# One of a seven-product pair's four weight sums moves to the narrow tile ahead of unit a, and units c and d exchange their contents

## The chip, the cores and the metric

One Trainium2 chip, one of its cores. The time is the device time of one execution in microseconds (us). Engines are named as in the profile: PE multiplies matrices (PEld loads its stationary operand), DVE is the vector engine, ACT the scalar engine, POOL the general one, SP issues the loads of the weights. All of them run their own queue of instructions in order and wait for one another through semaphores.

## The reference

A decoder trunk of two layers on 256 tokens with 2048 features: layer 0 mixes tokens by gated linear attention, layer 1 by differential attention over a shared K/V, and behind each stands a SwiGLU feed-forward. Nearly all the work is in products of the 256 tokens with large weights in float32. Cut to what matters here:

```python
def swiglu(h, w_gate_up, w_down):                     # (2048, 11264), (5632, 2048)
    gate, up = jnp.split(h @ w_gate_up, 2, axis=-1)
    return (jax.nn.silu(gate) * up) @ w_down
...
    for i in range(DEPTH):                            # 2
        h = rmsnorm(x, pre_mix_g[i])
        mix = gla_mixer(h, ...) if i < N_A_LAYERS else diff_mixer(h, k_sh, v_sh, ...)
        x = x + rmsnorm(mix, post_mix_g[i])
        f = swiglu(rmsnorm(x, pre_ffn_g[i]), ffn_w_gate_up[i], ffn_w_down[i])
        x = x + rmsnorm(f, post_ffn_g[i])
```

## The kernel before

**Weights as units.** Every weight reaches the core in blocks of 128x1024 floats (512 KB), two 512-column pieces of one output chunk side by side: rows k1 = 2s in the left half, rows k2 = 2s + 1 in the right. `load` (L256) brings a block into one of five `raw` buffers. `split` (L290) turns it into two tiles that PE multiplies at full rate: ACT casts it to `hi` (L294), DVE subtracts to get `lo` (L296). A product then takes three matmuls: hi by hi, hi by lo, lo by hi (`mm_act` L361, `triple` L438). Nine `hi` and `lo` buffers of the full width form a ring, so conversion runs ahead of PE by up to nine units.

**Pairs.** Two output chunks c1, c2 of the same weight are computed together by `duo_act` (L446, gated linear attention) and `duo_apart` (L485, elsewhere). At the steps s listed in `FAST_...` (L40 to L44) the eight block products of two token halves, two row blocks and two column chunks are replaced by seven. Such a step loads two blocks, r1 (chunk c1) and r2 (chunk c2), and feeds PE four units: a (r1 as loaded, 2 products), b (sums in r2, 2 products), c (sums in r1, 2 products) and d (a tile of half width, 1 product). With L and R for the halves, the sums that `sums` (L310) writes are, in order: r1L = r1L + r2L; r2L = r2L + r2R; t2 = r1L + r2R; r1R = t2 + r1R. Unit c then holds (r1L + r2L) and the last sum, unit d holds t2 = r1L + r2L + r2R. There are 122 such pairs, 98 of them in the two feed-forwards. The products go to seven accumulators ("banks"): 4 belongs to r1L + r2L, 5 to r1L + r2L + r2R. Token forms that go with them are made once for each stage by `build_forms` (L538); `early` and `late` of each stage combine the banks.

**What sets the order.** `take` (L349) asks for units in the order of `weight_stream` (L81); `pump` (L342) converts ahead as far as the ring allows and then issues loads ahead, up to five blocks beyond those done with. A raw buffer is filled again when the last instruction that reads the block in it has finished, so a load waits in SP's queue for a `split` on DVE. `convert` (L325) calls `sums` when it comes to unit b. A scheduler then puts the instructions of each engine in a fixed order, by what it reckons to be ready first; it moves matmuls, splits and sums past one another. The tile t2 lay in the stage's own pool (`self.narrow[0]`), the half-width `hi` and `lo` of unit d in that pool or in two or three spare places (`room`).

Of the kernel before, what the change touches and what calls it, by code (L numbers as in the profile page):

```python
# [11 lines left out]
F32 = mybir.dt.float32  # L12
# [3 lines left out]
ALU = mybir.AluOpType  # L16
AX = mybir.AxisListType

P = 128
# [3 lines left out]
C = 512  # L23
# [163 lines left out]
class Trunk:  # L187
# [119 lines left out]
        )  # L307
        return hi

    def sums(self):  # L310

        nc = self.nc
        r1, r2 = self.pending
        t2 = self.narrow[0].tile([P, C], F32, tag="sum", name=self.uid("sum"))

        def add(out, in0, in1):
            nc.vector.tensor_tensor(out=out, in0=in0, in1=in1, op=ALU.add)  # L317

        add(r1[:, :C], r1[:, :C], r2[:, :C])
        add(r2[:, :C], r2[:, :C], r2[:, C:])  # L320
        add(t2, r1[:, :C], r2[:, C:])
        add(r1[:, C:], t2, r1[:, C:])
        self.pending = r1, r2, t2

    def convert(self):  # L325
        n = self.n_conv
        kind = self.stream[n][2]
        self.n_done += kind in ("plain", "beside", "c", "b")
        if kind == "plain":
            self.subs[n] = self.split(self.raw(), n in self.pool_lo) if n else self.split_halves(self.raw())  # L330
        elif kind == "beside":
            self.subs[n] = self.split_beside(self.raw())
        elif kind == "a":
            self.pending = self.raw(), self.raw()
            self.subs[n] = self.split(self.pending[0])
        else:
            if kind == "b":
                self.sums()
            self.subs[n] = self.split(self.pending["cbd".index(kind)])
        self.n_conv += 1  # L340

    def pump(self):  # L342
# [103 lines left out]
    def duo_act(self, aT, forms, fast, c1, c2, early, late):  # L446

        ps = [self.acc() for _ in range(6)] + [self.tp().rearrange("p j t -> p (j t)")]
        for s in range(8):
            k1, k2 = 2 * s, 2 * s + 1  # L450
            if s in fast:
                f = forms.pairs.index(s)
                plan = {
                    "a": ((0, (k1, 0)), (1, (k2, 0))),
                    "b": ((6, (f, 2)), (2, (f, 3))),
                    "c": ((4, (f, 0)), (3, (k2, 1))),
                    "d": ((5, (f, 1)),),
                }
                first, last = s == fast[0], s == fast[-1]
                for kind, prods in plan.items():  # L460
                    wp = self.take("duo", (c1, c2, s), kind)
                    for j, (bank, (i, which)) in enumerate(prods):
                        plain = kind == "a" or bank == 3
                        a = aT.tokens(i, which) if plain else forms.fast(i, which)
                        stop = last and bank in (0, 5, 6)
                        self.triple(ps[bank], a, wp, j, first, stop)
                    self.free()
                    if kind != "d":
                        self.tick()
                if last:  # L470
                    early(ps)
                continue
            for (w, n), pair in ((c1, ((1, 0), (3, 1))), (c2, ((4, 1), (2, 2)))):
                wp = self.take(w, (n, s))
                for bank, which in pair:
                    for j in range(2):
                        a = forms.diff(k1 + j) if which == 2 else aT.tokens(k1 + j, which)
                        self.triple(ps[bank], a, wp, j, False, s == 7 and j == 1)
                    if s == 7:
                        late(bank, ps)  # L480
                    if bank in (2, 3):
                        self.free()
                    self.tick()

    def duo_apart(self, aT, forms, fast, chunks, early, late):  # L485

        ps = {}

        def add(bank, a, wp, j, last):
            first = bank not in ps  # L490
            if first:
                ps[bank] = self.acc() if bank < 6 else self.tp().rearrange("p j t -> p (j t)")
            self.triple(ps[bank], a, wp, j, first, last)

        for s in range(8):
            k1, k2 = 2 * s, 2 * s + 1
            if s not in fast:
                for (w, n), banks in zip(chunks, ((1, 3), (2, 7))):
                    wp = self.take(w, (n, s))
                    for b, bank in enumerate(banks):  # L500
                        for j in range(2):
                            add(bank, aT.tokens(k1 + j, b), wp, j, s == 7 and j == 1)
                        if b:
                            self.free()
                        if s == 7:
                            late(bank, ps)
                        self.tick()
                continue
            f, last = forms.pairs.index(s), s == fast[-1]
            plan = {  # L510
                "a": ((0, aT.tokens(k1, 0)), (1, aT.tokens(k2, 0))),
                "b": ((6, forms.fast(f, 2)), (2, forms.fast(f, 3))),
                "c": ((4, forms.fast(f, 0)), (3, aT.tokens(k2, 1))),
                "d": ((5, forms.fast(f, 1)),),
            }
            for kind, prods in plan.items():
                wp = self.take("duo", (*chunks, s), kind)
                for j, (bank, a) in enumerate(prods):
                    add(bank, a, wp, j, last and bank in (0, 4, 5, 6))
                self.free()  # L520
                if kind != "d":
                    self.tick()
            if last:
                early(ps)
# [1059 lines left out]
```

## Time and profile before

| what | before |
|---|---|
| time, median of 3 runs (2179.7 to 2179.91) | 2179.7 us |
| span of the profiled execution | 2177.2 us |
| PE busy, matmuls | 99%, 10098 |
| PEld busy | 83% |
| DVE busy, instructions | 89%, 2646 |
| ACT busy | 58% |
| DMA engines' packets of the weight queue, share of 16 engines | 60.2% |
| mean granted clock of PE | 0.999 |

The span runs from the first to the last instruction of one profiled execution; the time of a run is about 2.5 us more. A row of the chain or of a group names a line of the kernel, an engine, an operation, "out<-in" by tile names without numbers, a count, the busy time and the mean duration. A matmul's duration in the trace contains its way through the array, so consecutive matmuls overlap: their starts tell the rate. DVE instructions overlap a little as well: one of 690 ns lets the next start 600 to 720 ns after it.

### The profile page before, as it was taken

Reading aid. Unit: us, or ns where it says so; the run is one execution under the profiler, and the core shown is the slowest. Engines: PE = TensorE matmul, PEld = TensorE weight load, DVE = VectorE, ACT = ScalarE, POOL = GpSimd, SP = SyncE. Lnnn points to the kernel's source line nnn. Section 1 sums busy time; section 2 is a strip of 40 time slices with the busy share of each in tenths; the row PEclk is TensorE's granted clock in tenths of the full one; section 3 lists DMA queues with packets and bytes.
Section 4 is the critical chain, followed back from the end, with each engine's and each line's share of the span. In section 5 each row is a group of like instructions: output and inputs, shape, how many; then the busy total and the mean of one; then the engine's idle time right before and its main releaser. Section 6 shows DMA issues by size and latency. Waiting matters only on the chain.

```text
span 2177.2 us, 28399 instructions
## 1 busy us (share of the span) xinstructions
PE 2162.6 (99%) x10098; PEld 1798.1 (83%) x10098; DVE 1932.7 (89%) x2646; ACT 1267.2 (58%) x1744; POOL 35.6 (2%) x66
## 2 busy tenths in 40 slices
PE   9999999999999999999999999999999999999998
PEld 8887788888888888888878888888888888888886
DVE  7989988998999999998898567889999999999986
ACT  8656665665655555554676455556566555555553
POOL 1000000000000000000000000000000000000000
PEclk9999999999999999999999999999999999999999
DMA  8545566666655566665757655465656555666664
GB/s 309 169 149 191 177 228 213 213 221 215 228 176 199 194 213 213 194 224 189 243 187 248 186 174 161 151 235 189 231 194 223 182 185 195 209 206 212 212 213 135
DMA packets 123315, 440.09 MB, mean 202 GB/s; under 512 B 13899, under 2 KB 16628, under 8 KB 121380
## 3 DMA queue, kind: packets, MB, share of 16 engines
q1 hardware_dynamic: 121996, 436.44, 60.2%
q10 hardware_dynamic: 1176, 1.84, 0.3%
q8 instruction: 79, 1.29, 0.2%
q14 instruction: 64, 0.52, 0.1%
HBM read 429.82 MB, written 9.97 MB: 202 GB/s over the span
## 4 chain that ended last, share of the span: by engine, by line
PE 96%; DVE 2%; DMA 1%; issue 1%; ACT 1%; POOL 0%; SPq 0%; DVEq 0%; POOLq 0%; ACTq 0%
PE acc L444 13%; PE acc L443 13%; PE acc L442 13%; PE acc L372 10%; PE acc L370 10%; PE acc L371 10%; PE acc L585 8%; PE acc L586 4%; PE tp L443 3%; PE tp L444 3%; PE tp L442 3%; PE tp L606 1%; DVE lo L296 1%; PE acc L1307 0%; PE acc L1346 0%
## 5 line engine op out<-in xcount | busy, mean ns | idle before, releaser
L294 ACT CAST hi<-raw 128x1024 fp32r<-128x1024 f32 x905 | 929.5, 1051 | 656.6 <-DVE raw L317 272.7
L296 DVE TENSOR_TENSOR lo<-raw,hi 128x1024 fp32r<-128x1024 f32 x903 | 1077.6, 1220 | 151.8 <-ACT hi L294 148.9
L370 PE MATMUL acc<-hi,f_ffn_gT 128*128 128x512 f32 x704 | 274.1, 390 | 0.0
L371 PE MATMUL acc<-lo,f_ffn_gT 128*128 128x512 f32 x704 | 274.0, 390 | 0.0
L372 PE MATMUL acc<-hi,f_ffn_gT 128*128 128x512 f32 x704 | 268.9, 389 | 0.0
L444 PE MATMUL acc<-hi,h_ffn 128*128 128x512 f32 x666 | 259.6, 390 | 0.0
L443 PE MATMUL acc<-lo,h_ffn 128*128 128x512 f32 x666 | 259.2, 389 | 0.0
L442 PE MATMUL acc<-hi,h_ffn 128*128 128x512 f32 x666 | 258.4, 390 | 0.0
L372 PEld LDWEIGHTS acc<-hi,f_ffn_gT 128*128 128x128 f32 x704 | 132.2, 188 | 27.3
L370 PEld LDWEIGHTS acc<-hi,f_ffn_gT 128*128 128x128 f32 x704 | 132.2, 188 | 27.2
L371 PEld LDWEIGHTS acc<-lo,f_ffn_gT 128*128 128x128 f32 x704 | 132.2, 188 | 27.0
L444 PEld LDWEIGHTS acc<-hi,h_ffn 128*128 128x128 f32 x666 | 125.0, 188 | 26.5 <-issue 0.6
L443 PEld LDWEIGHTS acc<-lo,h_ffn 128*128 128x128 f32 x666 | 125.1, 188 | 25.9
L442 PEld LDWEIGHTS acc<-hi,h_ffn 128*128 128x128 f32 x666 | 125.0, 188 | 25.9
L585 PE MATMUL acc<-h_q,hi 128*128 128x512 f32 x256 | 92.5, 401 | 0.0
L585 PE MATMUL acc<-h_kv,hi 128*128 128x512 f32 x256 | 90.6, 399 | 0.0
L585 PE MATMUL acc<-h_mix,hi 128*128 128x512 f32 x256 | 90.5, 398 | 0.0
L317 DVE TENSOR_TENSOR raw<-sum,raw 128x512 f32<-128x512 f32 x122 | 84.2, 690 | 3.5
L317 DVE TENSOR_TENSOR raw<-raw 128x512 f32<-128x512 f32 x122 | 84.2, 690 | 3.3
L317 DVE TENSOR_TENSOR raw<-raw,raw 128x512 f32<-128x512 f32 x122 | 83.9, 687 | 2.0
L317 DVE TENSOR_TENSOR sum<-raw,raw 128x512 f32<-128x512 f32 x122 | 83.5, 684 | 0.0
L586 PE MATMUL acc<-h_q,lo 128*128 128x256 f32 x256 | 73.2, 286 | 0.0
(416 smaller groups left out, 3912.4 us busy)
## 6 DMA issues: line engine op xcount, KB each, us to landing
raw<-in_w_gu_dram SPq DMA_DIRECT2D x352, 512.0 KB, 4.4
raw<-in_w_d_dram SPq DMA_DIRECT2D x176, 512.0 KB, 5.2
raw<-in_gla_w_r_dram SPq DMA_DIRECT2D x32, 512.0 KB, 4.4
raw<-in_gla_w_v_dram SPq DMA_DIRECT2D x32, 512.0 KB, 4.0
raw<-in_gla_w_out_dram SPq DMA_DIRECT2D x32, 512.0 KB, 4.5
raw<-in_w_v_dram SPq DMA_DIRECT2D x32, 512.0 KB, 4.7
raw<-in_w_k_dram SPq DMA_DIRECT2D x32, 512.0 KB, 4.0
raw<-in_diff_w_q_dram SPq DMA_DIRECT2D x32, 512.0 KB, 3.5
```

The lines of the kernel that those rows point to most:

```text
L294: nc.scalar.copy(hi, src)
L296: eng.tensor_tensor(out=lo, in0=src, in1=hi.bitcast(F32), op=ALU.subtract)
L317: nc.vector.tensor_tensor(out=out, in0=in0, in1=in1, op=ALU.add)
L370: nc.tensor.matmul(ps, ah, rh, start=(kt == 0), stop=False)
L371: nc.tensor.matmul(ps, ah, rl, start=False, stop=False)
L372: nc.tensor.matmul(ps, al, rh, start=False, stop=(kt == 2 * ns - 1))
L442: nc.tensor.matmul(ps, ah, wh, start=first, stop=False)
L443: nc.tensor.matmul(ps, ah, wl, start=False, stop=False)
L444: nc.tensor.matmul(ps, al, wh, start=False, stop=last)
L585: nc.tensor.matmul(ps, lh, aT.both(kt), start=(kt == 0), stop=False)
L586: nc.tensor.matmul(ps[:, SEQ:], ll, aT.hi(kt), start=False, stop=(kt == KT - 1))
L606: nc.tensor.transpose(tp[:, j, :], src[:, j * P : (j + 1) * P], self.ident)
```

## The change

`sums` is gone. `convert_fast` now makes the first sum when it comes to unit a, out of the place: t1 = r1L + r2L into a tile of half width, and only then splits r1. At unit b it makes r2L = r2L + r2R, r1L = t1 + r2R, r1R = r1L + r1R. So r1 then holds in its left half what t2 held, and the half-width tile holds r1L + r2L: unit c feeds bank 5 (and 3), unit d bank 4. The tile comes from the ring's pool, with one buffer for the whole kernel. The number of sums, splits, loads and matmuls stays as it was. What differs is the order, and which engine waits for what.

```diff
-    def sums(self):
-        nc = self.nc
-        r1, r2 = self.pending
-        t2 = self.narrow[0].tile([P, C], F32, tag="sum", name=self.uid("sum"))
...
-        add(r1[:, :C], r1[:, :C], r2[:, :C])
-        add(r2[:, :C], r2[:, :C], r2[:, C:])
-        add(t2, r1[:, :C], r2[:, C:])
-        add(r1[:, C:], t2, r1[:, C:])
-        self.pending = r1, r2, t2
+    def add(self, out, in0, in1):
+        self.nc.vector.tensor_tensor(out=out, in0=in0, in1=in1, op=ALU.add)
+
+    def convert_fast(self, kind):
+        if kind == "a":
+            r1, r2 = self.raw(), self.raw()
+            t1 = self.ring.tile([P, C], F32, tag="sum", name=self.uid("sum"), bufs=1)
+            self.pending = r1, r2, t1
+            self.add(t1, r1[:, :C], r2[:, :C])
+            return self.split(r1)
+        r1, r2, t1 = self.pending
+        if kind == "b":
+            self.add(r2[:, :C], r2[:, :C], r2[:, C:])
+            self.add(r1[:, :C], t1, r2[:, C:])
+            self.add(r1[:, C:], r1[:, :C], r1[:, C:])
+            return self.split(r2)
+        return self.split(r1 if kind == "c" else t1)
...
-        elif kind == "a":
-            self.pending = self.raw(), self.raw()
-            self.subs[n] = self.split(self.pending[0])
         else:
-            if kind == "b":
-                self.sums()
-            self.subs[n] = self.split(self.pending["cbd".index(kind)])
+            self.subs[n] = self.convert_fast(kind)
...
-                    "c": ((4, (f, 0)), (3, (k2, 1))),
-                    "d": ((5, (f, 1)),),
+                    "c": ((5, (f, 1)), (3, (k2, 1))),
+                    "d": ((4, (f, 0)),),
...
-                "c": ((4, forms.fast(f, 0)), (3, aT.tokens(k2, 1))),
-                "d": ((5, forms.fast(f, 1)),),
+                "c": ((5, forms.fast(f, 1)), (3, aT.tokens(k2, 1))),
+                "d": ((4, forms.fast(f, 0)),),
```

In the changed file the sums stand at L311, and most lines have moved up by one (L296 has not; L443 of before is L442). Three places show how the scheduled order differs. Tile numbers are kept in the rows; raw_2848 and raw_2851 are the blocks r1 and r2 of one fast step of layer 1's feed-forward, raw_2854 and raw_2857 the two blocks of the plain step behind it, and raw_2863 and raw_2871 are r1 and r2 of the next fast step.

DVE before, from the last sum of the first of these steps to the first sums of the next:

```order
L317 TENSOR_TENSOR raw_2848_14954<-sum_2868_15053,raw_2848_14954 128x512
L296 TENSOR_TENSOR lo_2870_15059<-raw_2851_14966,hi_2869_15058 128x1024
L296 TENSOR_TENSOR f_ffn1_rest_13223<-sum_2868_15053,f_ffn1_rest_13223 128x512
L296 TENSOR_TENSOR lo_2873_15077<-raw_2848_14954,hi_2872_15076 128x1024
L296 TENSOR_TENSOR lo_2880_15125<-raw_2854_14978,hi_2879_15124 128x1024
L609 TENSOR_TENSOR f_ffn1_gT2_14686<-tp_2875_15082,f_ffn1_gT2_14686 128x4x128
L609 TENSOR_TENSOR f_ffn1_gT2_14686<-tp_2876_15089,f_ffn1_gT2_14686 128x4x128
L296 TENSOR_TENSOR lo_2883_15143<-raw_2857_14987,hi_2882_15142 128x1024
L296 TENSOR_TENSOR lo_2886_15163<-raw_2863_15015,hi_2885_15162 128x1024
L317 TENSOR_TENSOR raw_2863_15015<-raw_2863_15015,raw_2871_15062 128x512
```

DVE after, the same stretch:

```order
L311 TENSOR_TENSOR raw_2848_14954<-sum_2864_15033,raw_2851_14966 128x512
L296 TENSOR_TENSOR lo_2870_15059<-raw_2851_14966,hi_2869_15058 128x1024
L311 TENSOR_TENSOR raw_2848_14954<-raw_2848_14954 128x512
L296 TENSOR_TENSOR lo_2873_15077<-raw_2848_14954,hi_2872_15076 128x1024
L311 TENSOR_TENSOR sum_2885_15162<-raw_2863_15015,raw_2871_15062 128x512
L296 TENSOR_TENSOR lo_2880_15125<-raw_2854_14978,hi_2879_15124 128x1024
L296 TENSOR_TENSOR lo_2883_15143<-raw_2857_14987,hi_2882_15142 128x1024
L311 TENSOR_TENSOR raw_2871_15062<-raw_2871_15062 128x512
L296 TENSOR_TENSOR lo_2887_15165<-raw_2863_15015,hi_2886_15164 128x1024
L608 TENSOR_TENSOR f_ffn1_gT2_14686<-tp_2875_15082,f_ffn1_gT2_14686 128x4x128
L608 TENSOR_TENSOR f_ffn1_gT2_14686<-tp_2876_15089,f_ffn1_gT2_14686 128x4x128
```

The next step's first sum, which reads r2 = raw_2871, now stands ahead of the splits of the plain step (lo_2880, lo_2883) and of its own unit a; the split of unit d (f_ffn1_rest, not in the second list) has moved ahead of unit b's.

PE before at the same place, from the last matmul of unit a (lo_2865) on:

```order
L444 MATMUL acc_2895_15213<-hi_2864_15033,h_ffn1_0_13065 128x512
L442 MATMUL acc_2895_15213<-hi_2879_15124,h_ffn1_0_13065 128x512
L370 MATMUL acc_2866_15039<-hi_2849_14962,f_ffn1_gT2_14686 128x512
L371 MATMUL acc_2866_15039<-lo_2850_14963,f_ffn1_gT2_14686 128x512
L370 MATMUL acc_2877_15096<-hi_2855_14983,f_ffn1_gT2_14686 128x512
L371 MATMUL acc_2877_15096<-lo_2856_14984,f_ffn1_gT2_14686 128x512
L370 MATMUL acc_2867_15040<-hi_2849_14962,f_ffn1_gT2_14686 128x512
L371 MATMUL acc_2867_15040<-lo_2850_14963,f_ffn1_gT2_14686 128x512
L370 MATMUL acc_2878_15097<-hi_2855_14983,f_ffn1_gT2_14686 128x512
L371 MATMUL acc_2878_15097<-lo_2856_14984,f_ffn1_gT2_14686 128x512
L443 MATMUL acc_2895_15213<-lo_2880_15125,h_ffn1_0_13065 128x512
```

PE after (L605 are transposes, which before stand ahead of unit a):

```order
L443 MATMUL acc_2895_15213<-hi_2865_15035,h_ffn1_0_13065 128x512
L605 MATMUL tp_2875_15082<-ident_72,sg_2858_14989 128x128 x4
L605 MATMUL tp_2876_15089<-ident_72,sg_2858_14989 128x128 x4
L441 MATMUL acc_2895_15213<-hi_2879_15124,h_ffn1_0_13065 128x512
L441 MATMUL acc_2894_15209<-hi_2886_15164,h_ffn1_0_13065 128x512
L442 MATMUL acc_2895_15213<-lo_2880_15125,h_ffn1_0_13065 128x512
```

The first use of lo_2880 has moved ahead of eight matmuls on f_ffn1_gT2 and behind eight transposes.

The third place is the last head of differential attention. DVE before, from unit c of the first fast step of the output projection to the head's scores (s7):

```order
L296 TENSOR_TENSOR lo_2348_12378<-raw_2307_12181,hi_2347_12377 128x1024
L296 TENSOR_TENSOR lo_2369_12468<-sum_2346_12372,hi_2368_12467 128x512
L296 TENSOR_TENSOR lo_2361_12425<-raw_2304_12159,hi_2360_12424 128x1024
L1311 TENSOR_TENSOR s7_0_12397<-acc_2356_12394,bias7_12345 128x256
L1315 TENSOR_REDUCE st_2357_12399<-s7_0_12397 128x2
```

DVE after:

```order
L296 TENSOR_TENSOR lo_2348_12378<-raw_2307_12181,hi_2347_12377 128x1024
L296 TENSOR_TENSOR lo_2361_12425<-raw_2304_12159,hi_2360_12424 128x1024
L296 TENSOR_TENSOR lo_2371_12484<-raw_2313_12217,hi_2370_12483 128x1024
L311 TENSOR_TENSOR sum_2384_12538<-raw_2336_12319,raw_2349_12381 128x512
L311 TENSOR_TENSOR raw_2349_12381<-raw_2349_12381 128x512
L296 TENSOR_TENSOR lo_2376_12510<-raw_2326_12268,hi_2375_12509 128x1024
L1310 TENSOR_TENSOR s7_0_12397<-acc_2356_12394,bias7_12347 128x256
L1314 TENSOR_REDUCE st_2357_12399<-s7_0_12397 128x2
```

Two splits of plain blocks and two sums of the next fast step now stand ahead of the head's scores.

More of the change, by code (lines that the diff above doesn't have):

```diff
@@ L308, in split_beside @@
         return hi
-    def sums(self):
-        nc = self.nc
-        r1, r2 = self.pending
-        t2 = self.narrow[0].tile([P, C], F32, tag="sum", name=self.uid("sum"))
-        def add(out, in0, in1):
-            nc.vector.tensor_tensor(out=out, in0=in0, in1=in1, op=ALU.add)
-        add(r1[:, :C], r1[:, :C], r2[:, :C])
-        add(r2[:, :C], r2[:, :C], r2[:, C:])
-        add(t2, r1[:, :C], r2[:, C:])
-        add(r1[:, C:], t2, r1[:, C:])
-        self.pending = r1, r2, t2
+    def add(self, out, in0, in1):
[14 more added lines that the diff above has]
+        return self.split(r1 if kind == "c" else t1)
     def convert(self):
```

## Prediction

> **What bounds the kernel now.** The page's head comes first: the span, the busy time of each engine, and the chain of work that ended last.
>
> ```profile
> span 2177.2 us, 28399 instructions
> ...
> PE 2162.6 (99%) x10098; PEld 1798.1 (83%) x10098; DVE 1932.7 (89%) x2646; ACT 1267.2 (58%) x1744; POOL 35.6 (2%) x66
> ...
> PE 96%; DVE 2%; DMA 1%; issue 1%; ACT 1%; POOL 0%; SPq 0%; DVEq 0%; POOLq 0%; ACTq 0%
> ```
>
> PE is busy 99% and makes up 96% of the chain, but busy alone proves little, since consecutive matmuls overlap. So the waits of PE come next, the whole answer:
>
> ```profile
> PE acc L372 <- DVE h_ffn L647: 1.2, 4, 0.3
> PE acc L693 <- POOL ones L718: 1.1, 1, 1.1
> PE acc L370 <- ACT h_kv L645: 1.0, 1, 1.0
> PE acc L372 <- DVE h_kv L647: 0.9, 3, 0.4
> PE tp L641 <- DMA x_in<-in_x_dram: 0.7, 1, 0.7
> PE acc L370 <- ACT diff_oT L1370: 0.7, 1, 0.7
> PE acc L371 <- DVE lo L287: 0.2, 1, 0.2
> ```
>
> The columns are total, times and longest in us. All of PE's waits are 5.8 us, and only the last two rows have to do with weights or with work near a moved sum. No row names a `lo` of L296: PE never waits for a converted unit. That limits any gain to 5.8 us, most of which (norms, x, ones) the change doesn't touch. It limits no loss, so the question is whether DVE, which makes every `lo` in order, can now come late for PE.
>
> The stretch from 600 to 662.5 us, all of it feed-forward, shows how much DVE has in hand (columns: length, then busy time and count of PE, PEld, DVE, ACT, POOL, then clock, DMA share, GB/s):
>
> ```profile
> 600.00:662.50 62.50, 62.50 (x281) 51.84 (x281) 59.08 (x71) 35.02 (x39) 0.00 (x0) 1.00 0.60 201
> ```
>
> PE has no idle time at a granted clock of 1.00; DVE has 62.50 - 59.08 = 3.4 us.
>
> **Work removed and added: nothing, 0 us.** Four sums per pair before, four after. A unit carries as many matmuls as it did, and units c and d only exchange banks 4 and 5.
>
> ```profile
> L296 DVE TENSOR_TENSOR lo<-raw,hi 128x1024 fp32r<-128x1024 f32 x903 | 1077.6, 1220 | 151.8 <-ACT hi L294 148.9
> ...
> L317 DVE TENSOR_TENSOR raw<-raw,raw 128x512 f32<-128x512 f32 x122 | 83.9, 687 | 2.0
> ...
> L317 DVE TENSOR_TENSOR sum<-raw,raw 128x512 f32<-128x512 f32 x122 | 83.5, 684 | 0.0
> ```
>
> A sum takes 684 to 687 ns whether it writes over its input or into a tile of its own, so t1 out of place costs what the sum in place did: 122 times 3 ns, 0.4 us of DVE's time at the most, inside its idle time. The cast to `hi` of unit a no longer stands next to the sum that overwrites r1L, and ACT, which waits 272.7 us for such sums, waits less:
>
> ```profile
> ACT hi L294 <- DVE raw L317: 272.7, 84, 5.5
> ```
>
> ACT is 58% busy and absent from PE's list but for 1.7 us of other tiles; what it gains PE cannot use. I take 0.
>
> **The new wait.** t1 reads r2 before r1 is split, so DVE meets r2's transfer earlier by the splits that used to stand in between. Where r2 has only just been asked for, DVE stands, and every `lo` behind it is late. What counts is whether one of these is needed within the delay. A typical place, in the stretch above:
>
> ```profile
> 636.88 0.33 SPq L259 DMA_DIRECT2D raw<-in_w_gu_dram  x1
> ```
>
> ```profile
> 637.37 4.62 DVE L296 TENSOR_TENSOR lo<-raw,hi 128x1024 fp32r<-128x1024 f32 x4
> 642.03 0.69 DVE L317 TENSOR_TENSOR raw<-raw,raw 128x512 f32<-128x512 f32 x1
> ```
>
> r2 is issued at 636.88. With the 3.5 us that a single transfer takes (row of the next site) it is there at 640.4. Before, the first sum came at 642.0. In the changed order it stands behind the first of the four splits, at 637.37 + 4.62 / 4 = 638.5, and waits 1.9 us. By the same step on other pairs I find such a wait, 1.2 to 1.9 us, at some 40 of the 122, about one in each such stretch of feed-forward. One fits into the 3.4 us, and the unit behind it has time: the `lo` that DVE writes from 1692.83 on (below) is first read here, 16 us later.
>
> ```profile
> 1710.08 0.39 PE L443 MATMUL tp<-lo,f_ffn_fast 128*128 128x512 f32 x1
> ```
>
> So elsewhere I take 0.
>
> **The first place where it does not fit: 1690 us**, the first two places of the order lists. The load of r2 (raw_2871), how long it took to land, and DVE:
>
> ```profile
> 1694.09 0.33 SPq L259 DMA_DIRECT2D raw<-in_w_gu_dram  x1
> ```
>
> ```profile
> raw<-in_w_gu_dram SPq DMA_DIRECT2D x1, 512.0 KB, 3.5
> ```
>
> ```profile
> 1692.83 1.23 DVE L296 TENSOR_TENSOR lo<-raw,hi 128x1024 fp32r<-128x1024 f32 x1
> 1693.98 0.68 DVE L296 TENSOR_TENSOR f_ffn_rest<-sum,f_ffn_rest 128x512 fp32r<-128x512 f32 x1
> 1694.58 2.35 DVE L296 TENSOR_TENSOR lo<-raw,hi 128x1024 fp32r<-128x1024 f32 x2
> ```
>
> SP issues when unit b's split ends (1692.83 + 1.23 = 1694.06). The changed order has the same instructions ahead of that split's end and of unit c's (unit d's split has moved forward, one sum back, 0.60 us each to the next start), so the issue stays at 1694.09 and r2 lands at 1697.6. Unit c's `lo` starts at 1694.58 and takes half of the 2.35, some 1.14 to the next start; DVE then reaches t1 at 1695.72 and waits 1.9. Sum (0.65 to the next start) and split (1.22): lo_2880 is ready at 1697.6 + 0.65 + 1.22 = 1699.47. PE:
>
> ```profile
> 1697.62 0.39 PE L442 MATMUL acc<-hi,h_ffn 128*128 128x512 f32 x1
> 1697.85 0.39 PE L370 MATMUL acc<-hi,f_ffn_gT 128*128 128x512 f32 x1
> ...
> 1699.66 0.39 PE L443 MATMUL acc<-lo,h_ffn 128*128 128x512 f32 x1
> ```
>
> Before, the use is the L443 at 1699.66, eight matmuls after 1697.85, which gives 0.226 each. In the changed order these eight stand behind it, and one other matmul (on hi_2886) ahead, so PE gets there at 1699.66 - 1.81 + 0.23 = 1698.1, and waits 1699.47 - 1698.1 = **1.4 us**. Bounds: 0 if PE is late by then or r2 comes sooner, and 2.3 if r2 takes the 4.4 us that is the median over all such loads.
>
> ```profile
> raw<-in_w_gu_dram SPq DMA_DIRECT2D x352, 512.0 KB, 4.4
> ```
>
> The Trainium skill ("DMA: Bandwidth & Descriptors", section "Anatomy of one DMA", for transfers that GpSimd issues, while these come from SP) fits a transfer as a fixed 2.0 us plus bytes over 436 GB/s; for 512 KB that is an estimate of 3.2, and the stall would be 1.1. The trace's 3.5 decides. The same page's "Rules for kernel authors" says to issue a DMA early and wait on its semaphore late; a sum moved forward does the reverse of the second, and by that rule the time rises.
>
> **The second place: the last head of differential attention**, where two splits and two sums now stand ahead of the scores s7.
>
> ```profile
> 1386.77 0.42 DVE L1311 TENSOR_TENSOR s<-acc,bias 128x256 f32<-128x256 f32 x1 [0.99 <-PE acc L1307]
> ...
> 1390.30 1.22 DVE L296 TENSOR_TENSOR lo<-raw,hi 128x1024 fp32r<-128x1024 f32 x1
> ...
> 1392.15 1.22 DVE L296 TENSOR_TENSOR lo<-raw,hi 128x1024 fp32r<-128x1024 f32 x1 [0.30 <-ACT hi L294]
> ...
> 1393.88 0.48 DVE L1329 SCALAR_TENSOR_TENSOR s<-s,st 128x256 f32<-128x256 f32 x1
> ```
>
> ```profile
> 1396.90 0.38 PE L1337 MATMUL tp<-ident,s 128*128 128x128 f32 x2
> ```
>
> ```profile
> 1407.90 0.50 PE L370 MATMUL acc<-hi,diff_oT 128*128 128x512 f32 x1 [0.68 <-ACT diff_oT L1370]
> ```
>
> What now stands ahead of s7 takes 1.14 + 0.60 + 0.60 + 1.14 = 3.5; the d split that stood there (0.60) is among what comes later. The 0.99 of idle time in front of s7 takes up about that much, leaving s7 some 2.4 late. Two splits leave the stretch up to the probabilities, with 0.30 of idle time (2.57); a d split and an a split (0.60 + 1.14 = 1.74) enter. So the last probabilities end at 1393.88 + 0.48 + 2.4 - 2.57 + 1.74 = 1395.9, and PE transposes them at 1396.90: **0**. If no idle time is taken up, 1.3 more makes them 0.3 late, and with another split of 1.14 ahead 1.4, which with the order's uncertainty I round to +1.8; in the other direction the wait of 0.68 goes.
>
> **The sum.** 1.4 + 0 + 0 = +1.4. Against the profiled span: 2177.2 + 1.4 = 2178.6. A run is 2179.7, 2.5 more than that span, which the change leaves: **2181.1 us**. The bounds: 2179.7 - 0.7 = 2179.0 below; 1.4 + 1.8 = 3.2 and two further places like the first (2.8) give 2185.7 above.
>
> **Rivals.**
>
> DVE becomes the bound (slower). In a feed-forward stretch it has 3.4 us, and 20 such stretches of 62.5 us make up the two feed-forwards. If two pairs of a stretch wait 1.9 each, 3.8 is over 3.4, nothing is caught up, the lead of nine units shrinks, and PE loses 0.4 per stretch: 8 us, 2187.7. With three waits it is 5.7 - 3.4 = 2.3, 46 us. For it: 89% DVE, and late splits free raw buffers late, so that the next r2 is issued late too; SP's loads wait for just these splits. Against: of before's idle time a part is waiting for ACT's casts, which run beside r2's transfer and shrink the 3.8; the stretch above has one such wait, not two. The point is 3.4 us of new waits per stretch. Chance 0.15.
>
> Nothing reaches PE: r2 lands sooner at the first place, or PE is itself later there. 2179.7, with the 0.68 gone 2179.0. Chance 0.13.
>
> Several tight places at once, without a lasting lack: four or more like the first, 1.4 times 4 = 5.6, 2185.3. Chance 0.05.
>
> DVE's order is what binds, and the change mends it (faster). DVE waits for ACT's casts:
>
> ```profile
> DVE lo L296 <- ACT hi L294: 148.9, 158, 4.6
> ```
>
> If t1 fills such a wait in each of 122 pairs, 122 times 0.687 = 84 us of DVE's waiting is covered, and a time that followed DVE would fall to some 2096. Against: PE has no wait for `lo` to give up, and matmuls start 0.226 apart. Chance 0.03. The Trainium skill ("Perfetto Trace Analysis", "Identifying the Most-Contended Engine") calls matmul busy time no measure and takes the busy share of weight loads, here 83% against DVE's 89%; by it DVE is the most contended engine and this rival the forecast. The trace disagrees, as its list of PE's waits is empty of DVE's splits.
>
> The change does not do what it says: the scheduler might put the sum back. The order lists show t1 ahead of unit a at the places read; chance nil.
>
> **How the numbers follow.** The forecast has 0.64. A measurement of this kernel tells about 0.2%, 4.4 us, from no change. Slower by more (over 2184.1): the DVE rival 0.15, several places 0.05, and 0.02 of the forecast's own upper end, 0.22. Faster by more (under 2175.3): 0.03 and 0.01 of the forecast for what I have not seen, 0.04. Within: 0.74. The range runs from 2178.0 (the lower bound of 2179.0, less a microsecond of PE's untouched waits) to 2188.0, the DVE rival with two waits; left out are that rival with three, and the faster one.
>
> **What would show it.** Right: PE's waits gain one row, "acc L442 <- DVE lo L296" (L442 is L443 of before), once, about 1.4 us near 1698; DVE waits on the DMA of raw ahead of sums, 1.2 to 1.9 each, some 40 times; ACT's wait of 272.7 for sums shrinks; between 600 and 662.5 PE stays at 62.50 with DVE under it. Wrong: PE waiting for `lo` in many feed-forward stretches (the DVE rival); the row at 1698 missing (nothing reaches PE); or a wait at the last head, about 1397, or at 1407.9 much above 0.68, where I put 0.

## The result

The changed kernel takes 2197.68 us (median of 4 runs, 2194.81 to 2199.28) against 2179.7 before: a ratio of 1.0082, 95% interval 1.0070 to 1.0094. It is 18 us slower; the prediction was 1.4 us slower, in a range that ended at 2188.

The head of the page of the changed kernel, as quoted of before:

```profile
span 2195.7 us, 28311 instructions
...
PE 2167.0 (99%) x10098; PEld 1797.5 (82%) x10098; DVE 1919.9 (87%) x2646; ACT 1266.4 (58%) x1744; POOL 37.5 (2%) x66
...
PE 77%; DVE 13%; DMA 4%; issue 3%; ACT 2%; POOL 0%; DVEq 0%; SPq 0%; ACTq 0%; POOLq 0%
```

The span grew by 18.5 us with the same counts of matmuls and of DVE and ACT instructions, and slightly less DVE time. The busy share of PE still reads 99% and says nothing; the chain that ended last does: of PE's 96% of before only 77% are left, and DVE and the DMA transfers have 17%. PE's waits (total, times, longest), the four rows that lead the answer:

```profile
PE tp L441 <- ACT f_mix_fast L546: 3.6, 1, 3.6
PE acc L442 <- DVE lo L296: 3.6, 6, 0.9
PE acc L369 <- ACT f_ffn_gT L607: 2.6, 4, 1.1
PE acc L441 <- ACT hi L294: 1.9, 2, 1.4
```

None of these was there before. They are few and short: 13 waits, 11.7 us. And the waits of DVE and of ACT:

```profile
DVE lo L296 <- ACT hi L294: 169.4, 176, 3.7
...
DVE sum L311 <- DMA raw<-in_w_gu_dram: 9.7, 21, 0.8
...
DVE sum L311 <- DMA raw<-in_gla_w_r_dram: 5.2, 8, 1.3
```

```profile
ACT hi L294 <- DVE raw L311: 381.3, 152, 4.9
ACT f_ffn_rest L294 <- DVE sum L311: 87.2, 39, 3.5
```

ACT's waits for sums in `raw` did not shrink from 272.7 us, they grew by 109; those for the sum of unit d, 20.8 us before, are 87.2; and DVE's waits for ACT's casts grew from 148.9 to 169.4. The waits for r2's transfer are there, but small: none above 1.3 us.

To see where the 18.5 us lie, I took from each trace the distance between the starts of consecutive matmuls, less what is usual for their shape, and summed it by place:

| place | changed kernel against before, us |
|---|---|
| output projection of gated linear attention (near 327 us) | +6.2 |
| feed-forward of layer 0 | +4.0 |
| last head of differential attention | +1.7 |
| feed-forward of layer 1 | +7.3 |
| the rest | -0.8 |

**The place at 1690 us** (1710 in the changed kernel) shows what happens in the feed-forwards. PE, DVE and ACT there:

```profile
1710.16 0.50 PE L441 MATMUL acc<-hi,h_ffn 128*128 128x512 f32 x1
1712.05 0.51 PE L441 MATMUL acc<-hi,h_ffn 128*128 128x512 f32 x1 [1.39 <-ACT hi L294]
1712.89 0.50 PE L442 MATMUL acc<-lo,h_ffn 128*128 128x512 f32 x1 [0.33 <-DVE lo L296]
```

```profile
1705.45 0.68 DVE L311 TENSOR_TENSOR raw<-sum,raw 128x512 f32<-128x512 f32 x1
1706.18 1.23 DVE L296 TENSOR_TENSOR lo<-raw,hi 128x1024 fp32r<-128x1024 f32 x1
1707.32 0.68 DVE L311 TENSOR_TENSOR raw<-raw 128x512 f32<-128x512 f32 x1
1709.19 1.23 DVE L296 TENSOR_TENSOR lo<-raw,hi 128x1024 fp32r<-128x1024 f32 x1 [1.19 <-ACT hi L294]
1711.01 0.69 DVE L311 TENSOR_TENSOR sum<-raw,raw 128x512 f32<-128x512 f32 x1 [0.59 <-DMA raw<-in_w_gu_dram]
1711.62 2.35 DVE L296 TENSOR_TENSOR lo<-raw,hi 128x1024 fp32r<-128x1024 f32 x2
```

```profile
1705.09 1.05 ACT L294 CAST hi<-raw 128x1024 fp32r<-128x1024 f32 x1 [2.57 <-DVE raw L311]
1708.11 3.89 ACT L294 CAST hi<-raw 128x1024 fp32r<-128x1024 f32 x4 [1.97 <-DVE raw L311]
```

Read the DVE rows in order: the sum r1L, the split of unit b (1706.18), and only then the pair's last sum, r1R = r1L + r1R (1707.32). Unit c holds r1R, so ACT's cast of c, which could follow the cast of b at 1706.1, waits 1.97 us for that sum. ACT's next three casts stand behind it, those of the two plain units and of the next unit a, whose blocks have long been there: they end at 1712.0, and PE waits 1.39 us for one. DVE in turn has nothing between the last sum and unit c's split, waits 1.19 us for the cast, then 0.59 us for r2, and comes late with the next `lo`, for which PE waits 0.33 us. Before, all four sums stood together ahead of unit b's split. DVE's last sum there, and ACT's casts of b, of d and then of c and the unit behind it:

```profile
1692.22 0.69 DVE L317 TENSOR_TENSOR raw<-sum,raw 128x512 f32<-128x512 f32 x1
```

```profile
1691.75 1.05 ACT L294 CAST hi<-raw 128x1024 fp32r<-128x1024 f32 x1 [4.39 <-DVE raw L317]
1692.70 0.61 ACT L294 CAST f_ffn_rest<-sum 128x512 fp32r<-128x512 f32 x1
1693.22 1.99 ACT L294 CAST hi<-raw 128x1024 fp32r<-128x1024 f32 x2
```

DVE's split of b (1.23 us from 1692.83 on) and of d (0.68) ran beside these casts; ACT, once past its wait for the sum of unit b, went on without another, and neither DVE nor PE waited. So one sum that stands 1.2 us further back makes two engines wait for each other. Most pairs of the feed-forwards stand in the new order (80 of 98: of the 101 in the table below, 21 stand elsewhere); PE loses time at nine places besides this one.

### The profile page after: what moved, and what is told of

Same layout as the page of the kernel before. It is cut to its first block, busy times and chain, and to the rows that moved or that the text cites. A ratio compares the mean times of both kernels' runs of the same rounds, so it can differ in the third digit from the quotient of the medians.

```text
span 2195.7 us, 28311 instructions
## 1 busy us (share of the span) xinstructions
PE 2167.0 (99%) x10098; PEld 1797.5 (82%) x10098; DVE 1919.9 (87%) x2646; ACT 1266.4 (58%) x1744; POOL 37.5 (2%) x66
## 4 chain that ended last, share of the span: by engine, by line
PE 77%; DVE 13%; DMA 4%; issue 3%; ACT 2%; POOL 0%; DVEq 0%; SPq 0%; ACTq 0%; POOLq 0%
PE acc L442 10%; PE acc L443 10%; PE acc L441 10%; PE acc L371 8%; PE acc L369 8%; PE acc L370 8%; PE acc L584 8%; DVE lo L296 6%; PE acc L585 4%; DMA raw<-in_w_d_dram 2%; PE tp L441 2%; PE tp L442 2%; PE tp L443 2%; DVE raw L311 2%; DMA raw<-in_w_gu_dram 1%
## 5 line engine op out<-in xcount | busy, mean ns | idle before, releaser
L294 ACT CAST hi<-raw 128x1024 fp32r<-128x1024 f32 x905 | 920.6, 1050 | 634.4 <-DVE raw L311 381.3
L296 DVE TENSOR_TENSOR lo<-raw,hi 128x1024 fp32r<-128x1024 f32 x903 | 1082.0, 1220 | 171.3 <-ACT hi L294 169.4
L369 PE MATMUL acc<-hi,f_ffn_gT 128*128 128x512 f32 x704 | 272.7, 390 | 2.6 <-ACT f_ffn_gT L607 2.6
L442 PE MATMUL acc<-lo,h_ffn 128*128 128x512 f32 x666 | 259.9, 390 | 3.3 <-DVE lo L296 3.3
L443 PE MATMUL acc<-hi,h_ffn 128*128 128x512 f32 x666 | 258.9, 389 | 0.0
L441 PE MATMUL acc<-hi,h_ffn 128*128 128x512 f32 x666 | 253.8, 391 | 1.4 <-ACT hi L294 1.4
L311 DVE TENSOR_TENSOR raw<-raw 128x512 f32<-128x512 f32 x244 | 167.5, 687 | 2.8
L442 PEld LDWEIGHTS acc<-lo,h_ffn 128*128 128x128 f32 x666 | 125.0, 188 | 30.7 <-DVE lo L296 5.1
L443 PEld LDWEIGHTS acc<-hi,h_ffn 128*128 128x128 f32 x666 | 125.1, 188 | 25.6
L294 ACT CAST f_ffn_rest<-sum 128x512 fp32r<-128x512 f32 x98 | 60.7, 619 | 93.0 <-DVE sum L311 87.2
L311 DVE TENSOR_TENSOR sum<-raw,raw 128x512 f32<-128x512 f32 x122 | 83.9, 687 | 18.8 <-DMA raw<-in_w_gu_dram 9.7
L311 DVE TENSOR_TENSOR raw<-sum,raw 128x512 f32<-128x512 f32 x122 | 83.4, 684 | 0.0
```

What stands on the lines that cost most here:

```text
L294: nc.scalar.copy(hi, src)
L296: eng.tensor_tensor(out=lo, in0=src, in1=hi.bitcast(F32), op=ALU.subtract)
L311: self.nc.vector.tensor_tensor(out=out, in0=in0, in1=in1, op=ALU.add)
L369: nc.tensor.matmul(ps, ah, rh, start=(kt == 0), stop=False)
L441: nc.tensor.matmul(ps, ah, wh, start=first, stop=False)
L442: nc.tensor.matmul(ps, ah, wl, start=False, stop=False)
```

## The experiments

Three theories were set against each other. **Wait**: DVE stands for r2's transfer, as predicted, only more often. **Chain**: the last sum stands behind unit b's split, as just read. **Order**: t1 and unit d's split simply take their 0.6 us each ahead of work that PE needs sooner.

What the scheduler made of each kernel explains the times, so for each pair the DVE order was counted for two things: whether the last sum stands behind unit b's split, and whether anything reads r2 ahead of unit a's split. Losses are against before, summed by place as above, from the profiled execution.

| kernel | time, us (median) | ratio to before, 95% | last sum behind b's split | r2 read ahead of a's split | output projection | both feed-forwards | last head |
|---|---|---|---|---|---|---|---|
| before | 2179.5 to 2179.8 | | 0 of 122 | 0 | | | |
| changed | 2197.68 | 1.0070 to 1.0094 | 101 | 105 | 6.2 | 11.3 | 1.7 |
| 1 t1 behind a's split | 2181.25 | 0.9998 to 1.0017 | 0 | 0 | 0.0 | 0.1 | 1.0 |
| 2 sums together | 2183.84 | 1.0009 to 1.0027 | 0 | 122 | 4.4 | 0.2 | 1.0 |
| 3 before, r2 touched first | 2184.91 | 1.0014 to 1.0034 | 0 | 122 | 0.0 | 7.7 | 1.2 |
| 4 t1 without r2 | 2199.59 | 1.0076 to 1.0106 | 114 | 105 | 2.0 | 16.7 | 0.3 |
| 5 as 1, output projection alone | 2200.53 | 1.0080 to 1.0110 | 98 | 102 | 5.7 | 12.5 | 1.7 |
| 6 as 2, and 1 in the output projections | 2180.51 | 0.9996 to 1.0015 | 0 | 114 | 0.0 | 0.2 | 1.0 |
| 7 as 2, feed-forwards alone | 2184.89 | 1.0016 to 1.0037 | 21 | 121 | 5.9 | 0.2 | 1.7 |
| 8 before, last sum behind b's split | 2233.98 | 1.0233 to 1.0263 | 122 | 0 | 1.6 | 48.6 | 0.3 |
| 9 as 1, feed-forwards alone | 2185.36 | 1.0016 to 1.0035 | 21 | 23 | 7.3 | 0.0 | 1.7 |
| 10 as 1, all but feed-forwards | 2197.28 | 1.0068 to 1.0102 | 79 | 82 | 0.0 | 11.7 | 1.0 |
| 11 as 1, v and r weights alone | 2198.94 | 1.0076 to 1.0110 | 90 | 94 | 6.6 | 11.4 | 1.7 |

The column of pairs that decides the feed-forwards is the fourth. Where it is 0, or 21 with all of these outside the feed-forwards, they lose 0.0 to 0.2 us, whatever the fifth says; the one exception is the third kernel, in which DVE is made to wait. The split of unit d, the other half of the order theory, can be told from the same orders: it stands ahead of unit b's split in 8 pairs before, in 113 of the changed kernel and in 121 of the first and second experiments, whose feed-forwards lose 0.1 and 0.2 us. So its place is not the cause there either.

The experiments use an order edge: `issue_after(x)` makes what is built inside it stand behind x on x's engine. It adds no work and no semaphore. Where a sum is written in the program has no such effect: with t1's line moved behind unit a's split in the text, or into unit b, DVE's scheduled order is the same in every row (so neither was run). What freed t1 to move is its tile of its own: the sum in place could not stand ahead of unit a's split, which still reads r1L.

**1. t1 behind unit a's split.**

```diff
-            self.add(t1, r1[:, :C], r2[:, :C])
-            return self.split(r1)
+            sub = self.split(r1)          # split keeps its DVE instruction in last_lo
+            with self.tc.issue_after(self.last_lo.ins):
+                self.add(t1, r1[:, :C], r2[:, :C])
+            return sub
```

> The changed kernel with one order edge added: t1 may stand on DVE only behind the split (lo) of unit a. Banks, tile and number of sums stay as changed. In the scheduled order all sums of a pair then stand together again ahead of unit b's split, as they did before. Wait theory (DVE stands for r2's transfer), chain theory (the last sum stands behind unit b's split, so ACT's cast of c comes late and DVE waits for it) and order theory (t1 and unit d's split take 0.6 us each ahead of work that PE needs sooner) all say 2179 to 2183, with PE's waits down from about 21 us to 6 to 9. If instead the exchange of units c and d or the one-buffer tile costs the time, it stays at 2193 to 2199.

2181.25 us: 16.4 of the 18 us are gone, and the interval of the ratio holds 1. PE makes up 96% of the chain again. The exchange of units c and d and the one-buffer tile cost nothing that can be measured; the order does. By itself this doesn't say what in the order, since the edge both puts t1 back and brings the sums together again (0 in the fourth column). ACT's waits for sums are long here too, 149.7 us in `raw` and 179.6 for unit d, more than the 293.5 before, so their total alone tells nothing of the time.

**2. The sums together, t1 still early.**

```diff
-            self.add(r1[:, C:], r1[:, :C], r1[:, C:])
-            return self.split(r2)
+            done = self.add(r1[:, C:], r1[:, :C], r1[:, C:])
+            with self.tc.issue_after(done.ins):
+                return self.split(r2)
```

> The changed kernel with one order edge added: unit b's split may stand on DVE only behind the pair's last sum. t1 stays early, so DVE still reads r2 early. Chain theory: 2180 to 2185, with DVE's waits for ACT's casts back from 169 to about 150 us and ACT's waits for sums clearly under 381. Wait theory: 2192 to 2199, since DVE's waits for raw transfers ahead of t1 (18.4 us in the changed kernel) stay. Order theory: 2190 to 2197, above all the stall of 3.75 us near 327 stays.

2183.84 us, as the chain theory said. In all 122 pairs DVE now reads r2 ahead of unit a's split, and its waits for raw transfers are about as large as in the changed kernel (20.3 us against 18.4 in all, 7.4 against 9.7 in the gate-and-up products), but it waits less for casts and ACT less for sums:

```profile
DVE lo L296 <- ACT hi L294: 133.1, 152, 2.1
...
DVE sum L311 <- DMA raw<-in_gla_w_r_dram: 9.9, 6, 2.4
DVE sum L311 <- DMA raw<-in_w_gu_dram: 7.4, 15, 1.9
```

```profile
ACT hi L294 <- DVE raw L311: 225.6, 135, 4.9
```

The feed-forwards lose 0.2 us in place of 11.3. So the early wait for r2, up to 1.9 us here as the prediction had it, is covered there; the chain is what cost. What is left stands at the last head and near 327 us, where the order theory expected the whole stall to stay and 2.0 us of it did:

```profile
PE tp L442 <- ACT f_mix_fast L547: 2.0, 1, 2.0
```

**3. The wait alone, in the kernel before.**

```diff
+            st = self.ring.tile([P, 1], F32, tag="touch", name=self.uid("touch"), bufs=2)
+            seen = self.nc.vector.tensor_copy(st, self.pending[1][:, :1])
+            with self.tc.issue_after(seen.ins):
-            self.subs[n] = self.split(self.pending[0])
+                self.subs[n] = self.split(self.pending[0])
```

> The kernel before, with a read of one column of r2 on DVE ahead of each pair's unit a (its result is not used): DVE must see r2 landed before it splits r1, nothing else changes in the sums or units. 122 reads of about 0.06 us are 7 us of DVE's time, inside its 244 us of idle time. Wait theory: 2190 or more, as this wait comes even earlier than the changed kernel's. Chain and order theories: 2179 to 2184.

2184.91 us, between the two expectations. A forced wait costs something, 7.7 us in the feed-forwards. DVE's wait at the touches there:

```profile
DVE touch L336 <- DMA raw<-in_w_gu_dram: 25.7, 25, 1.8
```

That is a mean of 1.0 us where t1 in the changed kernel waits 9.7 us over 21 times, 0.5 each. The wait is a real price, but not the one that the feed-forwards of the changed kernel pay: those of the second experiment keep waits of nearly that size and lose 0.2 us.

**4. t1 without r2.**

```diff
-            self.add(t1, r1[:, :C], r2[:, :C])
+            self.add(t1, r1[:, :C], r1[:, C:])
```

> The changed kernel, but t1 adds the right half of r1 in place of the left half of r2, so t1 needs no r2 (the product of the fast pairs is then not the reference's). t1 stays early and out of place; the first reader of r2 is unit b's first sum. Wait theory: 2179 to 2184, and no wait of DVE for a transfer ahead of a t1. Order theory: 2190 to 2199, as early sums and early splits of unit d remain. Chain theory: as the changed kernel, 2192 to 2199, where the last sum still stands behind unit b's split.

2199.59 us, just above the 2199 at which both the order and the chain theory ended. This one was meant to take the wait away and did not: the sum r2L of unit b moved ahead of unit a's split too, so r2 is still read there in 105 pairs.

```profile
DVE raw L311 <- DMA raw<-in_w_gu_dram: 25.9, 43, 2.7
```

With 114 last sums behind unit b's split and longer waits for r2 than in the changed kernel (25.9 us against 9.7), it can't tell the chain from the wait; all it shows is that the loss stays when t1 itself needs no r2.

**5 and 6. The output projections.** The edge of the first experiment where the pair's weights are those of an output projection, in the changed kernel (5) and in the second experiment (6, both projections).

```diff
-            self.add(t1, r1[:, :C], r2[:, :C])
-            return self.split(r1)
+            if self.loads[self.n_used - 1][0] not in ("gla_w_out",):    # 6: ("gla_w_out", "diff_w_out")
+                self.add(t1, r1[:, :C], r2[:, :C])
+                return self.split(r1)
+            (as in 1)
```

> The changed kernel with the edge of the first experiment (t1 behind unit a's split) only for the output projection of gated linear attention. In the trace of the changed kernel PE loses 6.0 us there: stalls of 0.45 and 3.75 near 326 and 327, and some 1.8 in slower matmuls behind them. If the losses of the places are separate: 2197.7 - 6.0 = 2191.7, between 2190 and 2194, with the feed-forward stalls as they are. If DVE is short of time throughout, so that what is won at one place is lost again at a later one: 2195 to 2199.

> The second experiment (sums together) with, besides, t1 behind unit a's split in the two output projections. The second experiment keeps 2.15 us of stall and some 1.4 us of slower matmuls near 327, and 1.6 us more than before at the last head. If the places are separate: 2183.8 - 3.5 - 1.6 = 2178.7, between 2178 and 2181; t1 then still stands ahead of unit a in the feed-forwards, at no cost. If early reads of r2 cost time by themselves: 2182 to 2186.

The sixth came out as expected, 2180.51 us: t1 ahead of unit a's split in 114 pairs costs nothing that can be measured once the sums stand together and the output projections have their edge. The fifth missed: 2200.53, above both of its ranges, with the wait still there.

```profile
PE tp L446 <- ACT f_mix_fast L551: 3.7, 1, 3.7
```

The reason can be read in the order. f_mix_fast is cast from adds that make the token forms of this projection, twenty instructions on DVE among its sums and splits. Ahead of the tenth of the adds on f_mix stand 183 sums and splits of weights before (the splits of unit d that go to a spare place are not counted), 187 in the changed kernel, and still 187 in the fifth; 186 in the second, 182 in the first and sixth. The edge in one stage doesn't bring them down when the pairs of the stage before have put their work in front.

**7. Sums together in the feed-forwards alone.** The edit is shown against the second experiment.

```diff
+            if not self.loads[self.n_used - 1][0].startswith("w_gu"):
+                return self.split(r2)
             with self.tc.issue_after(done.ins):
                 return self.split(r2)
```

> The changed kernel with unit b's split behind the last sum in the gate-and-up products of the two feed-forwards alone. Chain theory: the feed-forward stalls of the changed kernel, 3.7 us in the first and 6.7 in the second, go; 2197.7 - 10.4 = 2187.3, between 2185 and 2190, and the 6.0 us near 327 stay. Wait theory: 2193 to 2199, as t1 still reads r2 early.

2184.89 us, 0.1 under the range: by the sums of the table the feed-forward loss that goes is 11.1 and not 10.4. A stretch of the second feed-forward in the changed kernel, then the same in this one (columns as in the prediction):

```profile
1700.00:1762.50 62.50, 60.78 (x271) 49.81 (x270) 55.53 (x68) 33.64 (x38) 0.00 (x0) 1.00 0.56 186
```

```profile
1700.00:1762.50 62.50, 62.50 (x282) 51.85 (x281) 58.76 (x71) 35.09 (x39) 0.00 (x0) 1.00 0.58 202
```

In the same 62.5 us PE has 282 matmuls where the changed kernel has 271, and no idle time, with DVE doing more and not less. The 5.9 us near 327 stay.

**8. The chain alone, in the kernel before.** Its last sum is built behind unit b's split, with an order edge; no sum stands ahead of unit a's split.

```diff
-        add(r1[:, C:], t2, r1[:, C:])
...
+            if kind == "b":
+                r1, r2, t2 = self.pending
+                with self.tc.issue_after(self.last_lo.ins):
+                    self.nc.vector.tensor_tensor(out=r1[:, C:], in0=t2, in1=r1[:, C:], op=ALU.add)
```

> The kernel before, with its last sum (r1R) made to stand behind unit b's split on DVE; the other three sums, banks and tiles as before, no sum ahead of unit a. Chain theory: slower than before, 2184 to 2192: ACT casts unit c later, and DVE waits for it unless unit d's split (0.6 us) or another stands between, so less than the 10.4 us of the feed-forward stalls may come. Wait theory and order theory: 2179 to 2182.

2233.98 us, 54 slower than before and far above the range. The direction is that of the chain theory: with every last sum behind unit b's split (122 against 101), with no sum early and no early read of r2, the kernel loses time, DVE's waits for casts have the largest value of any kernel here, and PE waits for casts:

```profile
DVE lo L296 <- ACT hi L294: 208.3, 296, 3.2
```

```profile
PE tp L445 <- ACT hi L294: 9.4, 8, 1.5
```

But the scheduler also rearranged much else in this kernel, and no run separates that from the chain. So the 54 us are no measure of the chain in the changed kernel, and that the chain alone is enough is made likely here, not shown.

**9 and 10. The first experiment by stage**: the edge in the gate-and-up products alone (9), and everywhere but there (10).

> The changed kernel with the edge of the first experiment (t1 behind unit a's split) in the gate-and-up products of both feed-forwards alone; by the scheduled order the last sum stands behind unit b's split in 21 pairs, against 101 of 122 in the changed kernel. Chain theory: the feed-forward stalls go and the losses near 327 and at the last head stay, as with the seventh experiment (2184.9): 2184 to 2188. If early sums by themselves cost time in the feed-forward too, it lies clearly under the seventh: 2180 to 2183.

> The reverse of the ninth: the edge everywhere but in the gate-and-up products. The last sum stands behind unit b's split in 79 pairs, all of them in the feed-forwards. Chain theory: the feed-forward stalls stay, some 10 us, on the first experiment's 2181.3: 2189 to 2194. For the loss near 327, which the edge in the output projection alone (fifth experiment) did not remove: if it hangs on what the pairs of the stage before leave DVE to do, it is gone here (no wait for f_mix_fast above 1 us); if it stays, 2194 to 2200.

The ninth gives 2185.36, with the feed-forwards at 0.0: the same as the seventh, though t1 stands behind unit a's split in one and ahead of it in the other. That settles the feed-forwards: t1's place does not count there, the last sum's does. The tenth shows the reverse: the feed-forwards lose 11.7 us with nothing done to them, and the loss near 327 is gone:

```profile
PE tp L446 <- ACT f_mix_fast L551: 0.6, 1, 0.6
```

Its median, 2197.28, is above the range; the profiled execution, with 15.3 us in all, is the lowest of its four (2194.18 to 2200.94). Its runs spread by 6.8 us and the changed kernel's by 4.5, where the first experiment's spread by 2.8, so sums of single executions are good to a few us only where PE stalls. The mean granted clock goes with it: 0.999 in the profiled execution of the tenth, 0.997 in its three others, which were 1.1 to 6.8 us slower. The last section has what a stretch at half the clock costs; how many the other executions had was not traced.

**11. The pairs of the v and r weights alone.**

> The changed kernel with the edge (t1 behind unit a's split) only in the pairs ahead of the output projection of gated linear attention, those of its v and r weights. In the scheduled order of DVE, 188 sums and splits stand ahead of the tenth of the adds on f_mix (the token forms of that projection's second half), against 187 in the changed kernel and the fifth experiment, 186 in the second, which all lose time near 327, and 183 before and 182 in the first and tenth, which don't. Order theory (what stands ahead of the forms sets when they are ready): the wait for f_mix_fast stays, 3 us or more, and the time lies between 2195 and 2201. If the pairs of the v and r weights by themselves make the loss: no wait for f_mix_fast above 1 us, 2189 to 2194.

2198.94 us, in the range of the order theory, though not by the wait that it named. PE waits there for a cast of weights, for the matmul that stands just ahead of the first one on the form, and then hardly for the form:

```profile
331.11 0.80 PE L446 MATMUL acc<-hi,gla_oT 128*128 128x512 f32 x1 [3.74 <-ACT hi L294]
```

The loss of the place, 6.6 us, is the same. So neither the edge in the projection (5) nor in the pairs ahead of it (11) removes it, and both together do (1, 10). All kernels with 186 to 188 sums and splits ahead of the tenth add lose time there, 2.0 us (the fourth) to 7.3, and those with 182 or 183 none; the eighth, reordered throughout, has 179 and loses 1.6. That is as far as this goes: no run moved these sums and nothing else, so the cause of the loss near 327 stays open.

## Why the prediction was wrong

- **What bounds the kernel**: right. PE had next to nothing to gain, and the loss is PE waiting for units and forms.
- **Work removed and added, 0 us**: right; 1919.9 us of DVE against 1932.7, and the sums at 684 to 687 ns as before.
- **"ACT, which waits 272.7 us for such sums, waits less"**: wrong, and this is the step that failed. It looked at unit a alone. The order list of the prediction's own place shows the last sum behind unit b's split (`lo_2870`), and the text passed over it as "one sum back, 0.60 us each": counted in DVE's time, that is nothing. Counted through ACT it is a cast that starts after unit b's split and three casts queued behind it. ACT waits 381.3 us and, for unit d, 87.2 in place of 20.8. With the sums put together again, and t1 left early, the feed-forwards lose 0.2 us in place of 11.3 (second experiment).
- **The new wait**: the mechanism exists and was too large. Forecast were some 40 waits of 1.2 to 1.9 us; there are 34 in all (the two rows above and five more of smaller stages), 18.4 us together, the longest 1.3. In the stretch from 600 to 662.5 DVE waits for no transfer, and PE stays at 62.50, as forecast.
- **1690 us, +1.4**: the right place, and 2.3 us by the starts of matmuls, the upper bound. That it fits is luck, as the reason is another. Of the 1.9 us of waiting for r2, 0.59 came; 1.19 went to ACT's cast, which the sum did not contain. The expected row, `lo` late, has 0.33 us, and the larger one, 1.39, is a late `hi`.
- **The last head, 0 (bounds -0.7 to +1.8)**: +1.7, just under the upper bound; the idle time of 0.99 in front of the scores was not taken up as assumed (1.0 in the changed kernel). No run separates what makes this loss.
- **Elsewhere 0**: mis-sized by most of the loss. The feed-forwards lose 9 us beside the place at 1690, most of it at nine places of 0.2 to 1.3 us; the output projection 6.2, at a place that the prediction did not look at and whose cause stays open.
- **Rivals**: nearest was "several tight places at once", put at 0.05 and 2185.3. Its chance was far too small: the sums of every pair were rescheduled alike, and the prediction followed the order at three places only. That DVE becomes the bound did not come about: its condition was 3.4 us of new waits for r2 in each stretch of 62.5 us, and there are 9.7 us in both gate-and-up products together. For the faster rival, of the two measures for PE in the section cited there of the Trainium skill ("Perfetto Trace Analysis", "Identifying the Most-Contended Engine"), MFU and the busy share of weight loads, the prediction took the second alone, so that rule need not name DVE. The Trainium skill's rule to wait late for a DMA ("DMA: Bandwidth & Descriptors", "Rules for kernel authors") holds in direction, as the third experiment's 5 us show, but gives no account of the changed kernel.

## What to carry over

Where two in-order engines hand a tile back and forth (sum on DVE, cast on ACT, split on DVE), price a moved instruction by the other engine's queue and not by its own duration: ask what then starts later there, and what stands behind that. When a scheduler decides the order, compare the order around every step of the pattern, not only of the instruction that was meant to move; here the instruction that was meant to move cost some 4 us (second experiment), and the one that slipped back behind it cost 11 in the feed-forwards. An order edge put such an instruction back where it belongs at no cost that could be measured, and is also the cheapest experiment.

## What the hardware showed beside

A stall of PE near 327 us costs more than itself. The changed kernel:

```profile
331.51 0.50 PE L441 MATMUL tp<-hi,f_mix_fast 128*128 128x512 f32 x1 [3.58 <-ACT f_mix_fast L546]
...
332.69 0.63 PE L441 MATMUL acc<-hi,f_mix_fast 128*128 128x512 f32 x1
333.12 0.63 PE L442 MATMUL acc<-lo,f_mix_fast 128*128 128x512 f32 x1
...
335.25 0.63 PE L442 MATMUL acc<-lo,f_mix_fast 128*128 128x512 f32 x1
```

```profile
332.10:335.60 3.50, 3.50 (x10) 2.77 (x9) 3.05 (x5) 1.77 (x2) 0.00 (x0) 0.53 0.61 181
```

After the stall the first matmuls start 0.23 us apart as ever; from 332.3 on it is 0.43, for some 3.4 us, at a granted clock of 0.53: eight matmuls at 0.2 us more each, about 1.6 us on top of the stall. The Trainium skill ("TensorE: Matmul & The Clock Gate", "Part 1: The HAM clock gate") has a gate that halves the clock after an idle window of about 3.4 us and opens it after as long a busy one. The half rate and the 3.4 us agree; the idle time does not have to be that long, since in the second experiment a wait of 2.0 us was followed by the same (granted clock 0.53 over the next 3.4 us, the first row below), while the waits of 1.39 and 0.33 us at 1712 were not. Nor does the length decide alone: near 1094 us, waits of 2.21 and 0.43 us in the sixth experiment were followed by half the clock (second row), and waits of 2.16 and 0.42 us at the same place in the first were not (third row). So nearly the same stall can cost 1.6 us more or not; what decides between the two, no run here shows.

```profile
329.80:333.20 3.40, 3.40 (x9) 2.68 (x10) 3.40 (x6) 2.22 (x3) 0.00 (x0) 0.53 0.67 183
```

```profile
1095.40:1098.80 3.40, 3.40 (x9) 2.62 (x8) 3.40 (x9) 2.73 (x9) 0.00 (x0) 0.51 0.47 181
```

```profile
1095.10:1098.50 3.40, 3.19 (x16) 2.39 (x15) 3.40 (x9) 2.84 (x10) 0.00 (x0) 1.00 0.44 174
```
